# Unread transposes in the first blocks of the two feed-forward layers, with another order of products, splits from the bank and later norms of the memory

## Chip, cores and metric

The kernel runs on one core of a Trainium2 chip. The metric is the device time of one execution in microseconds (us). Before the change the median of three runs is 1266.1 us (1265.81 to 1266.46).

## What is computed

One layer of a streaming encoder over 512 tokens (batch 1) with 1024 channels, all in float32. The reference, cut to what matters:

```python
x = x + 0.5 * swiglu(rmsnorm(x, ffn1_norm), ffn1_wg, ffn1_wu, ffn1_wd)      # 1024 -> 2816 -> 1024
h = rmsnorm(x, mix_norm)
aq, ak, av, bq, bk, bv, cq = split(h @ w_in)
o_a = diff_attention(...)            # 4 heads, block-causal
o_b = chunk_band_attention(...)      # 8 heads, band of chunks
mk, mv = split(rmsnorm(mem, mem_norm) @ w_mem_kv)     # 256 memory tokens
o_c = memory_attention(rmsnorm(cq), rmsnorm(mk), mv)
y = sum_i sigmoid(h @ w_gate + b_gate)_i * (o_i @ w_branch_i)
x = x + y @ w_out
x = x + 0.5 * swiglu(rmsnorm(x, ffn2_norm), ffn2_wg, ffn2_wu, ffn2_wd)
x = rmsnorm(x, final_norm)
# swiglu(h, wg, wu, wd) = (silu(h @ wg) * (h @ wu)) @ wd
```

## The kernel before, in words

**Three matmuls for one.** Every float32 operand is split into a rounded part (`hi`, a cast on ACT, L77) and the rest (`lo`, a subtraction on DVE, L78). `split` (L75) issues both. A product is then three matmuls on TensorE (PE): hi by hi, lo by hi, hi by lo. So each 128x1024 block of weights costs one ACT cast and one DVE subtraction before PE can finish with it.

**Seven products for eight.** The two up-projections of a feed-forward layer (`ffn`, L346) go by Strassen-Winograd: for a pair of 128-wide slices of wg and wu (an `Item`, L376) and the two halves of the tokens there are seven products of half the size, named 1 to 7. `mm7` (L364) is one of them: 24 matmuls of 256 columns (L373) in two halves j of 12. The weight operand of products 5, 6, 7 and 3 is a sum or difference of weight blocks (`quarter`, made on DVE in `prep`, L390). The token operand is M1 to M7, made once per layer: M1 and M2 are the first 256 tokens (two halves of the channels), the others need the last 256 tokens too. Product 6 accumulates in bank s on top of product 1, then 7, then 4; product 5 goes into bank p or o (`z`), and 3 on top of it. Between them ACT copies bank s out (`snap`, L415 to L418), DVE adds (`cc`, L422), ACT applies silu (`sg`, L431), DVE multiplies (`pr`, L433), and `done` (L435) splits the gated result into `gh` and `gl`.

**The tokens at the start of a layer.** `Operands.rows` (L191) takes one tile of 128 tokens: a reciprocal root on POOL (`rsqrt`, L117), two norm halves on DVE (`xn`, L141), eight transposes on PE into two banks t (L201), and two ACT copies to `raw` (L202). For tiles 0 and 1, `combine` (L205) splits raw into M1 and M2; for tiles 2 and 3 it makes half of M6 (L220, L221 on DVE and a split). `need` (L225) makes M5, M7, M4 and M3 at the first product that wants them. In ffn1, `raw` lies in the tiles `gh` and `gl`, which is why rows of the first block name them.

**Order.** A scheduler sets the order on each engine from the order in which the code issues. `run_jobs` (L334) issues products and slices of the down-projection as jobs: `prep` (DVE, ACT, loads) runs ahead of the product by up to six weight blocks. The 22 slices of the hidden width go in chunks of 4, 6, 6 and 6 (L470), each of them up-projection and then down-projection (`mms`, L503), and `run_jobs` is called for every chunk (L536). PE's order is held only within one job, so the scheduler may mix matmuls of neighbouring jobs. The first block of a layer (chunk 0, first item) goes 1, 2, 1', 2', 6, 5, 7, 4, 3, 6', 5', 7' (the second item's products have a dash).

**The start and the memory.** 32 transposes of the identity that nobody reads (L279 to L281) keep PE at work before the first tokens come. `mem_rows` (L551) loads the 256 memory tokens, norms and transposes them; the scheduler takes loads and norms of it into ffn1's first block. After ffn1, `rows_product` (L584) forms mk, cq and mv; mk's product and mv's take the two banks s in turn, `norm4` (L604) norms mk from its bank on DVE with a root on POOL, and `heads_T` (L611) transposes it. Products with `w_u` of the next stage are prepared in the same time (`wlo` 128x768).

Of the kernel before, what the change touches and what calls it, by code (L numbers as in the profile page):

```python
# [32 lines left out]
PLAN_C0 = "p2 c.qt p2 c.sc p2 f4 c.sc2 p3 f2 c.qt f2 c.pt f4 c.pv"  # L33
# [5 lines left out]
WARM = 32  # L39

# [7 lines left out]
def layer_kernel(ctx: ExitStack, tc: tile.TileContext, a: dict, out: bass.AP):  # L48
# [103 lines left out]

    def norm_T(src, ss, gain, h, t):

        ms = tiny("ms", 1)
        nc.vector.tensor_scalar(out=ms, in0=ss[:, 0:1], scalar1=EPS, scalar2=ss[:, 1:2], op0=ALU.add, op1=ALU.add)
        rs = rsqrt(ms)
# [27 lines left out]
    class Operands:  # L185
# [5 lines left out]
        def rows(self, src, ss, gain, t):  # L191
            ms = tiny("ms", 1)
            nc.vector.tensor_scalar(out=ms, in0=ss[:, 0:1], scalar1=EPS, scalar2=ss[:, 1:2], op0=ALU.add, op1=ALU.add)
            rs = rsqrt(ms)
            xn = scratch("xn")
            for dh in range(2):
                norm_half(xn, src, rs, gain, dh)
                ps = bank("t")
                for k in range(4):
                    c = (dh * 4 + k) * P  # L200
                    nc.tensor.transpose(ps[:, k * P:(k + 1) * P], xn[:, c:c + P], ident)  # L201
                nc.scalar.copy(out=self.raw[dh][:, :, t * P:(t + 1) * P], in_=k4(ps))  # L202
            self.combine(t)

        def combine(self, t):  # L205
            M, (r0, r1) = self.M, self.raw
# [6 lines left out]
            if t < 2:  # L213
                part(1, r0[:, :, cols], cols)
                part(2, r1[:, :, cols], cols)
                return
# [27 lines left out]
    def squares(src):  # L244
        ss = tiny("ss", 2)
        dump = scratch("sq")
        for dh in range(2):
            d = slice(dh * 512, dh * 512 + 512)
            square_half(src[:, d], dump[:, d], ss[:, dh:dh + 1])
        return ss  # L250
# [11 lines left out]
    for t in range(NT):  # L262
        nc.sync.dma_start(out=x_sb[:, t, :], in_=x_v[:, t, :])
        if t == 0:
            gain1 = load_gain("ffn1_norm")
        elif t < 3:
            w1_raw.append(load(a["ffn1_w1"][0, t - 1], 1024))
# [10 lines left out]

    warm = bank("s")  # L279
    for _ in range(WARM):  # L280
        nc.tensor.transpose(warm[:, 0:P], ident, ident)  # L281
# [46 lines left out]
    class Job:  # L328


        def __init__(self, prep, run, blocks=1):
            self.prep, self.run, self.blocks = prep, run, blocks
# [12 lines left out]

    def ffn(pre, x_sb, ops, fp, after, raws=None, before_last=None, after_half=None):  # L346
# [17 lines left out]
        def mm7(ps, blk, m, first):  # L364

            for j in range(2):
                c = slice(j * HS, (j + 1) * HS)
                for k in range(4):
                    o = slice((j * 4 + k) * P, (j * 4 + k + 1) * P)
                    st, mv = tuple(w[:, o] for w in blk), tuple(v[:, k, :] for v in M[m])  # L370
                    for n, (x, y) in enumerate(((st[0], mv[0]), (st[0], mv[1]), (st[1], mv[0]))):

                        nc.tensor.matmul(ps[:, c], lhsT=x, rhs=y, start=first and j + k + n == 0,  # L373
                                         stop=k == 3 and n == 2, skip_group_check=True)

        class Item:  # L376


            def __init__(self, ft, G, g0, raws):
                self.ft, self.G, self.g0 = ft, G, g0  # L380
                self.raws = list(raws or [])
                self.pr = [None, None]

# [6 lines left out]
            def prep(self, p):  # L390
# [4 lines left out]
                if p == 2:  # L395
                    return block(self.raw(1))
                if p == 6:
                    self.s1, self.s2 = quarter(), quarter()
                    add(out=self.s1, in0=self.raw(2), in1=self.raw(3), op=ALU.add)
                    add(out=self.s2, in0=self.s1, in1=self.raw(0), op=ALU.subtract)  # L400
                    return block(self.s2)
                if p == 5:
                    got = block(self.s1)
                    self.s4 = quarter()
                    add(out=self.s4, in0=self.raw(1), in1=self.s2, op=ALU.subtract)
                    return got
# [59 lines left out]
        def product(item, p):  # L466
            return Job(lambda: item.prep(p), lambda blk: item.run(p, blk))

        ft = 0
        for n, nf in enumerate(CHUNKS):  # L470
            last = n == len(CHUNKS) - 1
            G = [fp.tile([P, 6, S], F32R, tag=t, name=t) for t in ("gh", "gl")]
# [3 lines left out]
            if ft == 0:  # L476

                order += [(items[0], 1), (items[0], 2), (items[1], 1), (items[1], 2)]
            else:
                order += [(items[0], 1), (items[0], 2)]  # L480
            for i, item in enumerate(items):
                order += [(item, 6), (item, 5), (item, 7)]
                if i + 1 < len(items) and not (ft == 0 and i == 0):
                    order += [(items[i + 1], 1)]
                if ft == 0 and i == 0:
                    order += [(item, 4), (item, 3)]
                elif i + 1 < len(items):
                    order += [(item, 4), (item, 3), (items[i + 1], 2)]
            jobs = [product(*o) for o in order]
# [3 lines left out]
            for dh in range(2):  # L493
# [3 lines left out]
                def chunk(k, d=d):  # L497
# [11 lines left out]
                def banks(acc, dh=dh, z=z, other=other):  # L509
                    acc.extend(bank(t) for t in (("g", "g", "s", other) if dh == 0 else ("s", z, "g", "g")))  # L510

                if dh == 0 or not last:
# [8 lines left out]
                    for k in range(0, nf, 2):  # L521
                        jobs.append(Job(lambda k=k, chunk=chunk: chunk(k), lambda wc, k=k, run=run: run(wc, k)))
                        if dh == 0 and k == 0:
                            jobs += end
                else:
# [10 lines left out]
            run_jobs(jobs, RING)  # L536
# [9 lines left out]
    for t in range(NT):  # L546
        ops.rows(x_sb[:, t, :], squares(x_sb[:, t, :]), gain1, t)

    mix_in = {}

    def mem_rows():  # L551
# [9 lines left out]
        gain = load_gain("mem_norm")  # L561
        for t in range(NMT):
            mt = scratch("mt")
            nc.sync.dma_start(out=mt, in_=a["mem"][t * P:(t + 1) * P, :])
            norm_T(mt, squares(mt), gain, mix_in["mT"], t)
# [7 lines left out]
    ffn("ffn1", x_sb, ops, fp, row_mix, raws=w1_raw, before_last=mem_rows)  # L573
# [49 lines left out]
    mk_ps = rows_product([bank("s") for _ in range(NMT)], mT, a["w_mem_kv"], 0, **mem_w)  # L623
    for t in range(NMT):
        yn = mem_pool.tile([P, 512], F32, tag="mk", name="mk", bufs=3)
        sq = mem_pool.tile([P, 512], F32, tag="mk", name="mksq", bufs=3)
        heads_T(norm4(mk_ps[t], yn, sq, gck), mkT, slice(t * P, (t + 1) * P))
# [4 lines left out]
    for t in range(NT):  # L632
        sq = mem_pool.tile([P, 512], F32, tag="mk", name="cqsq", bufs=3)
        norm4(cq_ps[t], c_rows[:, t, :], sq, gcq)

    lam = mem_pool.tile([P, 512], F32, tag="mk", name="lam", bufs=3)
# [447 lines left out]
    def row_out(t, ss):  # L1084
        ms = tiny("ms", 1)
        nc.vector.tensor_scalar(out=ms, in0=ss[:, 0:1], scalar1=EPS, scalar2=ss[:, 1:2], op0=ALU.add, op1=ALU.add)
        rs = rsqrt(ms)
# [66 lines left out]
```

## Time and profile before

| | |
|---|---|
| median of three runs | 1266.1 us (1265.81 to 1266.46) |
| the profiled execution | 1268.73 us |
| its span, first to last instruction | 1266.9 us |
| PE busy | 1228.1 us, 97% |
| DVE busy | 843.0 us, 67% |
| ACT busy | 596.8 us, 47% |
| mean granted clock of PE | 0.986 of full speed |

A view of the trace counts from the span's first instruction. Busy time of PE is the time in which a matmul is under way, whether the clock is at full or at half speed; the granted clock (PEclk) says which. In a row of the timeline stand start, duration, engine, line, operation, output<-inputs and, in brackets, how long the engine had been idle before and what released it. Back-to-back matmuls overlap, so what one costs is the distance from its start to the next one's start.

### The profile page before, as it was taken

The numbers are of one execution on the slowest core, as the hardware profiler recorded it, in microseconds if no ns is written. First come the engines' busy times: TensorE is split into PE (matmuls) and PEld (weight loads), VectorE is DVE, ScalarE is ACT, GpSimd is POOL, SyncE is SP. The second block draws the span as 40 slices with busy tenths as digits, with TensorE's granted clock in tenths as the row PEclk, the third lists the DMA queues.
The fourth block names the chain that finished last, engine by engine and source line by source line (L and its number), as shares of the span: only waits on it lengthen the run. The fifth ranks groups of instructions, "written<-read, shape, count | busy, mean of one in ns | idle before, by whom it ended". The sixth has DMA issues, their size and how long they took to land.

```text
span 1266.9 us, 19640 instructions
## 1 busy us (share of the span) xinstructions
PE 1228.1 (97%) x7808; PEld 1119.2 (88%) x7808; DVE 843.0 (67%) x1377; ACT 596.8 (47%) x1115; POOL 106.2 (8%) x108
## 2 busy tenths in 40 slices
PE   7889999999999899999999999999989999999997
PEld 7779989989987799999999999888887998998996
DVE  7977667667664756667765664554697776766753
ACT  7534525435443455554554544442464452542543
POOL 1100000000000301111121121111000000000002
PEclk8899999999999899999999999999989999999999
DMA  6532423323333413212221321145143242332311
GB/s 222 174 103 82 135 84 107 127 79 122 102 123 117 123 39 109 88 42 84 88 88 54 93 88 38 63 146 186 34 135 115 70 134 97 101 125 76 123 44 67
DMA packets 53084, 127.57 MB, mean 101 GB/s; under 512 B 10112, under 2 KB 10624, under 8 KB 52992
## 3 DMA queue, kind: packets, MB, share of 16 engines
q1 hardware_dynamic: 52416, 125.27, 31.1%
q8 instruction: 61, 1.00, 0.3%
q10 hardware_dynamic: 576, 1.05, 0.2%
q14 instruction: 31, 0.25, 0.1%
HBM read 122.11 MB, written 4.19 MB: 100 GB/s over the span
## 4 chain that ended last, share of the span: by engine, by line
PE 91%; DVE 4%; ACT 1%; DMA 1%; POOL 1%; issue 1%; SPq 0%; POOLq 0%; DVEq 0%; ACTq 0%
PE ps_s L373 19%; PE ps_g L110 9%; PE ps_g L112 9%; PE ps_g L111 9%; PE ps_o L373 5%; PE ps_p L110 5%; PE ps_p L112 5%; PE ps_p L111 4%; PE ps_p L373 4%; PE ps_g L373 4%; PE ps_s L110 3%; PE ps_s L111 3%; PE ps_s L112 3%; PE ps_o L906 2%; PE ps_s L874 2%; PE ps_t L722 1%
## 5 line engine op out<-in xcount | busy, mean ns | idle before, releaser
L77 ACT CAST whi<-wraw 128x1024 fp32r<-128x1024 f32 (+1 forms) x120 | 119.1, 993 | 144.6 <-PE ps_s L373 74.1
L78 DVE TENSOR_TENSOR wlo<-wraw,whi 128x1024 fp32r<-128x1024 f32 (+1 forms) x120 | 137.9, 1151 | 67.8 <-ACT whi L77 65.1
L373 PE MATMUL ps_s<-mhi,whi 128*128 128x256 f32 x496 | 140.3, 283 | 8.1 <-ACT snap L417 7.9
L373 PE MATMUL ps_s<-mlo,whi 128*128 128x256 f32 x496 | 139.3, 281 | 0.0
L373 PE MATMUL ps_s<-mhi,wlo 128*128 128x256 f32 x496 | 138.3, 281 | 0.6 <-DVE wlo L78 0.6
L373 PEld LDWEIGHTS ps_s<-mhi,whi 128*128 128x128 f32 x496 | 94.6, 191 | 10.6 <-ACT snap L417 9.5
L77 ACT CAST whi<-quarter 128x1024 fp32r<-128x1024 f32 x54 | 56.8, 1052 | 96.4 <-PE ps_o L112 22.4
L373 PEld LDWEIGHTS ps_s<-mlo,whi 128*128 128x128 f32 x496 | 94.7, 191 | 0.9 <-DVE mlo L78 0.2
L373 PEld LDWEIGHTS ps_s<-mhi,wlo 128*128 128x128 f32 x496 | 94.5, 191 | 0.9 <-DVE wlo L78 0.8
L110 PE MATMUL ps_p<-whi,hh 128*128 128x384 f32 (+1 forms) x264 | 95.0, 360 | 0.0
L112 PE MATMUL ps_p<-whi,hl 128*128 128x384 f32 (+1 forms) x264 | 89.6, 340 | 0.0
L111 PE MATMUL ps_p<-wlo,hh 128*128 128x384 f32 (+1 forms) x264 | 89.0, 337 | 0.0
L78 DVE TENSOR_TENSOR wlo<-quarter,whi 128x1024 fp32r<-128x1024 f32 x54 | 66.0, 1222 | 23.9 <-ACT whi L77 23.9
L110 PE MATMUL ps_g<-hh,fh 128*128 128x512 f32 x192 | 78.1, 407 | 0.0
L112 PE MATMUL ps_g<-hh,fl 128*128 128x512 f32 x192 | 75.5, 393 | 0.1
L111 PE MATMUL ps_g<-hl,fh 128*128 128x512 f32 x192 | 74.9, 390 | 0.0
L859 DVE CAST kx<-ps_t 128x256 fp32r<-128x256 f32 x32 | 13.6, 425 | 84.6 <-PE ps_t L857 84.6
L121 POOL TENSOR_TENSOR rsh<-msh,mhalf 128x4 f32<-128x4 f32 x38 | 45.2, 1191 | 277.5 <-DVE msh L127 225.8
L78 DVE TENSOR_TENSOR fl<-wraw,fh 128x768 fp32r<-128x768 f32 x48 | 50.0, 1042 | 24.0 <-ACT fh L77 24.0
L77 ACT CAST fh<-wraw 128x768 fp32r<-128x768 f32 x48 | 39.9, 833 | 37.7 <-PE ps_g L111 22.4
L724 ACT COPY pT<-ps_t 128x512 f32<-128x512 f32 (+3 forms) x56 | 23.5, 452 | 69.3 <-PE ps_t L722 69.3
L110 PEld LDWEIGHTS ps_p<-whi,hh 128*128 128x128 f32 x264 | 50.4, 191 | 1.6
(416 smaller groups left out, 3691.7 us busy)
## 6 DMA issues: line engine op xcount, KB each, us to landing
wraw<-in_ffn_w SPq DMA_DIRECT2D x88, 512.0 KB, 3.8
wraw<-in_ffn_wd SPq DMA_DIRECT2D x44, 512.0 KB, 3.9
wraw<-in_w_u SPq DMA_DIRECT2D x32, 384.0 KB, 3.2
wraw<-in_w_gb SPq DMA_DIRECT2D x32, 384.0 KB, 3.1
wraw<-in_w_gf SPq DMA_DIRECT2D x16, 384.0 KB, 3.1
wraw<-in_w_mem_kv SPq DMA_DIRECT2D x8, 512.0 KB, 4.1
wraw<-in_w_out SPq DMA_DIRECT2D x8, 512.0 KB, 4.8
x_sb<-in_x SPq DMA_DIRECT2D x4, 512.0 KB, 7.0
```

What stands on the lines that cost most here:

```text
L77: nc.scalar.copy(out=hi, in_=raw)
L78: (engine or nc.vector).tensor_tensor(out=lo, in0=raw, in1=f32(hi), op=ALU.subtract)
L110: nc.tensor.matmul(ps, lhsT=st[0], rhs=mv[0], start=first, stop=False)
L111: nc.tensor.matmul(ps, lhsT=st[0], rhs=mv[1], start=False, stop=False)
L112: return nc.tensor.matmul(ps, lhsT=st[1], rhs=mv[0], start=False, stop=last)
L121: nc.gpsimd.tensor_tensor(out=rs, in0=ms, in1=mhalf[:, :n], op=ALU.pow)
L373: nc.tensor.matmul(ps[:, c], lhsT=x, rhs=y, start=first and j + k + n == 0, stop=k == 3 and n == 2, skip_group_check=True)
L722: nc.tensor.transpose(ps[:, j * P:(j + 1) * P], pt[:, j * P:(j + 1) * P], ident)
L724: nc.scalar.copy(out=pT[:, :n * P], in_=ps[:, :n * P])
L859: nc.vector.tensor_copy(out=un.kx[:, :, qs], in_=heads(p2[:, 0:256], 2))
L874: nc.tensor.matmul(out_, lhsT=q, rhs=k, start=j == 0, stop=j == 1)
L906: nc.tensor.matmul(o[:, vs], lhsT=pT[:, j * P:(j + 1) * P], rhs=un.v[:, j, vs], start=j == 0, stop=j == i)
```

## The change

1. `busy(ps, n)` issues n transposes of the identity into a bank that the next product overwrites. With `BUSY = 16` it stands after each of the first two token tiles of ffn1, and ahead of product 5 of the first item in both feed-forward layers.
2. For token tiles 0 and 1, M1 and M2 are split straight from the transposes' bank, and the copy to `raw` comes after it.
3. The sum of squares of a token tile is one ACT instruction of 1024 elements, not two of 512.
4. The first loads go x0, x1, gain, first weights, x2, second weights, x3; before, gain came ahead of x1.
5. The memory's norms become `mem_norms`, a job behind the products of chunk 1 that loads through the ring of weight buffers; `mem_rows` only transposes.
6. All chunks of a layer are one list of jobs under one written order for PE. The first block goes 1, 2, 1', 2', first half of 5, 6, second half of 5, 7, 6', 4, 3, 5', 7'. Product 1 of chunk 1 is put in behind the first jobs of chunk 0's down-projection. The last half of a chunk's down-projection takes its banks in another order.
7. In the memory's section mv's product goes to the banks t, mk's transposes stand behind it, and the scratch tiles have tags of their own. `PLAN_C0`, the table that mixes pieces of the next stage, has another order.

```diff
+    def busy(ps, n):
+        for _ in range(n):
+            nc.tensor.transpose(ps[:, 0:P], ident, ident)
...
         def rows(self, src, ss, gain, t):
...
-                nc.scalar.copy(out=self.raw[dh][:, :, t * P:(t + 1) * P], in_=k4(ps))
-            self.combine(t)
+                cols = slice(t * P, (t + 1) * P)
+                if t < 2:
+                    split(k4(ps), *(v[:, :, cols] for v in self.M[1 + dh]))
+                nc.scalar.copy(out=self.raw[dh][:, :, cols], in_=k4(ps))
+            if t >= 2:
+                self.combine(t)
...
     def run_jobs(jobs, ring):
         made = alive = 0
-        for n, job in enumerate(jobs):
-            while made < len(jobs) and (made <= n or alive + jobs[made].blocks <= ring):
-                alive += jobs[made].blocks
-                jobs[made].got = jobs[made].prep() if jobs[made].prep else None
-                made += 1
-            with tc.manual_schedule(engines={mybir.EngineType.PE}):
+        with tc.manual_schedule(engines={mybir.EngineType.PE}):
+            for n, job in enumerate(jobs):
+                while made < len(jobs) and (made <= n or alive + jobs[made].blocks <= ring):
+                    alive += jobs[made].blocks
+                    jobs[made].got = jobs[made].prep() if jobs[made].prep else None
+                    made += 1
                 job.run(job.got)
-            alive -= job.blocks
+                alive -= job.frees
...
+                elif p == "5a":
+                    self.z = bank("p" if self.ft // 2 % 2 else "o")
+                    busy(self.z, BUSY)
+                    mm7(self.z, blk, 5, True, (0,))
+                elif p == "5b":
+                    mm7(self.z, self.blk5, 5, False, (1,))
...
+                order += [(items[0], "5a"), (items[0], 6), (items[0], "5b"), (items[0], 7), (items[1], 6), (items[0], 4),
+                          (items[0], 3), (items[1], 5), (items[1], 7)]
...
+                    jobs.insert(hole, product(items[0], 1))
...
-                    acc.extend(bank(t) for t in (("g", "g", "s", other) if dh == 0 else ("s", z, "g", "g")))
+                    acc.extend(bank(t) for t in (("g", "g", "s", other) if dh == 0 else (z, "g", "g", "s")))
...
-            run_jobs(jobs, RING)
             ft += nf
...
+    with tc.manual_schedule(engines={mybir.EngineType.PE}):
+        for t in range(2):
+            ops.rows(x_sb[:, t, :], squares(x_sb[:, t, :]), gain1, t)
+            busy(warm, BUSY)
...
+    def mem_norms():
+        gain = load(a["mem_norm"].partition_broadcast(P), 1024)
+        mix_in["mn"] = []
+        for t in range(NMT):
+            mt = load(a["mem"][t * P:(t + 1) * P, :], 1024)
+            xn = scratch("mn")
+            rs = mean_rsqrt(squares(mt, xn))
+            for dh in range(2):
+                norm_half(xn, mt, rs, (gain[:, :512], gain[:, 512:]), dh)
+            mix_in["mn"].append(xn)
...
-        heads_T(norm4(mk_ps[t], yn, sq, gck), mkT, slice(t * P, (t + 1) * P))
+        mk.append(norm4(mk_ps[t], yn, sq, gck))
...
-    mv_ps = rows_product([bank("s") for _ in range(NMT)], mT, a["w_mem_kv"], 512, **mem_w)
+    mv_ps = rows_product([bank("t") for _ in range(NMT)], mT, a["w_mem_kv"], 512, **mem_w)
...
+    for t in range(NMT):
+        heads_T(mk[t], mkT, slice(t * P, (t + 1) * P))
```

Three places of the order. First, PE from the last slices of the output projection (bank s, `yh`) into the first product of ffn2 (`mhi`, `whi`), with the transposes of its token tiles (`norms`), before:

```order
L112 MATMUL ps_s<-whi,yl 128x512
L201 MATMUL ps_t<-ident,norms 128x128 x16
L373 MATMUL ps_s<-mhi,whi 128x256 x2
L373 MATMUL ps_s<-mlo,whi 128x256
L373 MATMUL ps_s<-mhi,wlo 128x256
```

and with the change (lines left out between the parts are matmuls of the same products):

```order
L113 MATMUL ps_s<-whi,yl 128x512
L207 MATMUL ps_t<-ident,norms 128x128 x8
L381 MATMUL ps_s<-mhi,whi 128x256
L381 MATMUL ps_s<-mlo,whi 128x256
L381 MATMUL ps_s<-mhi,wlo 128x256
...
L381 MATMUL ps_g<-mlo,whi 128x256
L207 MATMUL ps_t<-ident,norms 128x128 x8
L381 MATMUL ps_g<-mhi,wlo 128x256
...
L207 MATMUL ps_t<-ident,norms 128x128 x8
L381 MATMUL ps_s<-mhi,whi 128x256
```

Of the sixteen transposes that stood ahead of the first product, the eight of token tile 2 now stand behind all 24 matmuls of it and two of the next; tile 3's stand behind the second product.

Second, DVE in the same stretch (`raw` is the copy of the transposed tokens, `quarter` a sum of weights or of tokens), before, from the split of tile 1's M2 on:

```order
L78 TENSOR_TENSOR mlo<-raw_9405,mhi 128x4x128
L220 TENSOR_TENSOR raw_9404<-raw_9404 128x4x128
L141 SCALAR_TENSOR_TENSOR norms<-x_sb,rs,norms 128x512 x2
L221 TENSOR_TENSOR quarter<-raw_9405,raw_9404 128x4x128
L400 TENSOR_TENSOR quarter<-quarter,wraw 128x1024
L78 TENSOR_TENSOR mlo<-quarter,mhi 128x4x128
L405 TENSOR_TENSOR quarter<-wraw,quarter 128x1024
L220 TENSOR_TENSOR raw_9404<-raw_9404 128x4x128
L221 TENSOR_TENSOR quarter<-raw_9405,raw_9404 128x4x128
L78 TENSOR_TENSOR flo<-wraw,fhi 128x1024
```

and with the change:

```order
L79 TENSOR_TENSOR mlo<-ps_t,mhi 128x4x128 x2
L158 TENSOR_SCALAR ms<-sst 128x1
L142 SCALAR_TENSOR_TENSOR norms<-x_sb,rs,norms 128x512 x2
L226 TENSOR_TENSOR raw_9162<-raw_9162 128x4x128
L227 TENSOR_TENSOR quarter<-raw_9163,raw_9162 128x4x128
...
L226 TENSOR_TENSOR raw_9162<-raw_9162 128x4x128
L79 TENSOR_TENSOR wlo<-quarter,whi 128x1024
L227 TENSOR_TENSOR quarter<-raw_9163,raw_9162 128x4x128
L242 TENSOR_TENSOR raw_9162<-raw_9163,raw_9162 128x4x256
L79 TENSOR_TENSOR flo<-wraw,fhi 128x1024
```

The norm halves of tile 3 now stand ahead of tile 2's subtraction (L226), and `flo`, which the fourth product needs, stands behind one more split and one more subtraction of 1024 elements.

Third, DVE in the memory's section, where `mk` is the first read of mk's bank, `rsh` POOL's root, before:

```order
L78 TENSOR_TENSOR mwl<-wraw,mwh 128x1024
L127 TENSOR_SCALAR msh<-hss 128x4
L78 TENSOR_TENSOR wlo<-wraw,whi 128x768
L602 TENSOR_TENSOR mk<-ps_s,rsh 128x512
L600 TENSOR_REDUCE hss<-mksq 128x4
```

and with the change:

```order
L79 TENSOR_TENSOR wlo<-wraw,whi 128x768
L128 TENSOR_SCALAR msh<-hss 128x4 x2
L79 TENSOR_TENSOR mwl<-wraw,mwh 128x1024
L646 TENSOR_REDUCE hss<-cqsq 128x4
L648 TENSOR_TENSOR mk<-ps_s,rsh 128x512
```

PE no longer needs mk's bank for mv's product; it needs the splits `mwl` of mv's weights, of which the third stands here and the fourth six rows further, behind four of the norms.
## Rows read from the trace of the kernel before

**Rows 1.** The page: the span, and busy time (share) xinstructions of each engine

```profile
span 1266.9 us, 19640 instructions
...
PE 1228.1 (97%) x7808; PEld 1119.2 (88%) x7808; DVE 843.0 (67%) x1377; ACT 596.8 (47%) x1115; POOL 106.2 (8%) x108
```

**Rows 2.** Windows in us: their length, busy time (xstarts) by engine, PEclk, DMA, GB/s

```profile
1.30:6.50 5.20, 5.15 (x24) 5.15 (x25) 0.44 (x2) 2.04 (x5) 0.56 (x1) 1.00 0.88 267
6.50:8.00 1.50, 1.50 (x14) 1.31 (x13) 1.41 (x2) 0.08 (x1) 0.00 (x0) 1.00 1.02 418
10.00:20.00 10.00, 5.64 (x27) 5.02 (x28) 8.96 (x13) 10.00 (x21) 2.01 (x3) 0.67 0.83 320
30.00:40.00 10.00, 5.67 (x27) 4.60 (x26) 9.56 (x12) 5.40 (x9) 4.86 (x1) 0.70 0.35 106
412.70:419.60 6.90, 4.68 (x11) 3.78 (x12) 4.87 (x10) 1.20 (x2) 2.75 (x3) 0.51 0.48 167
920.00:930.00 10.00, 6.83 (x56) 6.63 (x55) 9.89 (x12) 8.69 (x11) 0.00 (x0) 0.91 0.16 52
930.00:940.00 10.00, 9.68 (x63) 9.47 (x62) 10.00 (x12) 4.79 (x6) 0.00 (x0) 0.75 0.50 159
```

**Rows 3.** PE's waits: releaser: us in total, times, longest

```profile
PE ps_s L110 <- DVE mk L602: 5.8, 1, 5.8
...
PE ps_o L373 <- DVE mlo L78: 3.5, 2, 3.2
```

**Rows 4.** Timeline of DVE in ffn1's first block: the memory's norms

```profile
34.91 1.42 DVE L141 SCALAR_TENSOR_TENSOR xn<-mt,rs,gain 128x512 f32<-128x512 f32 x2 [0.44 <-POOL rs L121]
...
44.44 1.42 DVE L141 SCALAR_TENSOR_TENSOR xn<-mt,rs,gain 128x512 f32<-128x512 f32 x2 [0.44 <-POOL rs L121]
```

**Rows 5.** Timeline of PE in ffn1's first block

```profile
35.81 1.94 PE L149 MATMUL ps_t<-ident,xn 128*128 128x128 f32 x8 [1.23 <-DVE xn L141]
38.12 0.58 PE L373 MATMUL ps_o<-mlo,whi 128*128 128x256 f32 x1 [0.36 <-DVE mlo L78]
...
41.05 0.28 PE L373 MATMUL ps_o<-mhi,whi 128*128 128x256 f32 x1
41.16 0.28 PE L373 MATMUL ps_o<-mlo,whi 128*128 128x256 f32 x1
```

**Rows 6.** Timeline of PE in the memory's section

```profile
414.92 0.77 PE L110 MATMUL ps_s<-mwh,mh 128*128 128x512 f32 x1 [5.78 <-DVE mk L602]
```

**Rows 7.** Timeline of DVE in the memory's section

```profile
412.22 0.96 DVE L78 TENSOR_TENSOR wlo<-wraw,whi 128x768 fp32r<-128x768 f32 x1
414.08 0.69 DVE L602 TENSOR_TENSOR mk<-ps_s,rsh 128x512 f32<-128x512 f32 x1 [0.91 <-POOL rsh L121]
```

**Rows 8.** Timeline of PE at the start of ffn2

```profile
913.41 0.38 PE L373 MATMUL ps_s<-mhi,whi 128*128 128x256 f32 x1 [0.23 <-ACT ps_s L137]
...
928.85 0.58 PE L373 MATMUL ps_o<-mlo,whi 128*128 128x256 f32 x1 [3.17 <-DVE mlo L78]
```

**Rows 9.** Timeline of DVE at the start of ffn2

```profile
914.50 0.69 DVE L220 TENSOR_TENSOR raw<-raw 128x512 f32<-128x512 f32 x1
915.10 1.41 DVE L141 SCALAR_TENSOR_TENSOR norms<-x_sb,rs,norms 128x512 f32<-128x512 f32 x2
...
921.30 1.22 DVE L78 TENSOR_TENSOR flo<-wraw,fhi 128x1024 fp32r<-128x1024 f32 x1
```

**Rows 10.** Timeline of ACT at the start of ffn2

```profile
913.76 1.08 ACT L202 COPY raw<-ps_t 128x512 f32<-128x512 f32 x2
```

**Rows 11.** Timeline of DVE at the end of ffn1's chunk 1

```profile
165.04 0.69 DVE L422 TENSOR_TENSOR cc<-ps_o,snap 128x512 f32<-128x512 f32 x1
...
166.78 0.69 DVE L78 TENSOR_TENSOR gl<-pr,gh 128x512 fp32r<-128x512 f32 x1
```

**Rows 12.** Timeline of ACT at the end of ffn1's chunk 1

```profile
165.49 0.62 ACT L77 CAST gh<-pr 128x512 fp32r<-128x512 f32 x1
166.01 0.41 ACT L431 ACTIVATE sg<-cc 128x256 f32<-128x256 f32 x1
```

More of the change, by code (lines that the diff above doesn't have):

```diff
@@ L191, in rows @@
         def rows(self, src, ss, gain, t):
-            ms = tiny("ms", 1)
-            nc.vector.tensor_scalar(out=ms, in0=ss[:, 0:1], scalar1=EPS, scalar2=ss[:, 1:2], op0=ALU.add, op1=ALU.add)
-            rs = rsqrt(ms)
+            rs = mean_rsqrt(ss)
             xn = scratch("xn")
@@ L242, in need, with squares @@
                 split(hi[1], *self.M[3])
[L244 to L249, printed above, removed]
+    def squares(src, dump=None):
+        ss = tiny("ss", 1)
+        square_half(src, scratch("sq") if dump is None else dump, ss)
         return ss
@@ L277, in layer_kernel @@
     nc.vector.memset(mhalf, -0.5)
+    def busy(ps, n):
+        for _ in range(n):
+            nc.tensor.transpose(ps[:, 0:P], ident, ident)
     warm = bank("s")
-    for _ in range(WARM):
-        nc.tensor.transpose(warm[:, 0:P], ident, ident)
+    busy(warm, WARM)
     def add_rows(x_sb, acc, t, dh, scale, after=None, after_half=None, sss={}):
@@ L362, in block, with mm7 @@
             return weight(None, 1024, fp, (("fhi", "flo"), ("ohi", "olo"))[n - 4], 1, raw=raw)
-        def mm7(ps, blk, m, first):
-            for j in range(2):
+        def mm7(ps, blk, m, first, parts=(0, 1)):
+            for j in parts:
                 c = slice(j * HS, (j + 1) * HS)
@@ L396, in prep @@
                     return block(self.raw(1))
+                if self.s1 is None:
+                    self.s1 = quarter()
+                    add(out=self.s1, in0=self.raw(2), in1=self.raw(3), op=ALU.add)
                 if p == 6:
-                    self.s1, self.s2 = quarter(), quarter()
-                    add(out=self.s1, in0=self.raw(2), in1=self.raw(3), op=ALU.add)
+                    self.s2 = quarter()
                     add(out=self.s2, in0=self.s1, in1=self.raw(0), op=ALU.subtract)
[L401 to L405, printed above, removed]
+                    got = block(self.s2)
+                elif p == 5:
+                    got = self.blk5 = block(self.s1)
+                if p in (5, 6):
+                    self.done56 += 1
+                    if self.done56 == 2:
+                        self.s4 = quarter()
+                        add(out=self.s4, in0=self.raw(1), in1=self.s2, op=ALU.subtract)
                     return got
@@ L435, in done @@
             def done(self, f):
+                if not self.G:
+                    self.G += [fp.tile([P, 6, S], F32R, tag=t, name=t) for t in ("gh", "gl")]
                 split(self.pr[f], *(v[:, self.g0 + f, :] for v in self.G))
@@ L466, in product @@
         def product(item, p):
+            if p == "5a":
+                return Job(lambda: item.prep(5), lambda blk: item.run(p, blk), 1, 0)
+            if p == "5b":
+                return Job(None, lambda blk: item.run(p, blk), 0, 1)
             return Job(lambda: item.prep(p), lambda blk: item.run(p, blk))
         ft = 0
+        jobs = []
         for n, nf in enumerate(CHUNKS):
             last = n == len(CHUNKS) - 1
-            G = [fp.tile([P, 6, S], F32R, tag=t, name=t) for t in ("gh", "gl")]
+            G = []
             items = [Item(ft + i, G, i, raws if ft + i == 0 else None) for i in range(0, nf, 2)]
@@ L475, in ffn @@
             order = []
-            if ft == 0:
+            if n == 0:
                 order += [(items[0], 1), (items[0], 2), (items[1], 1), (items[1], 2)]
-            else:
[L480 to L489, printed above, removed]
+                order += [(items[0], "5a"), (items[0], 6), (items[0], "5b"), (items[0], 7), (items[1], 6), (items[0], 4),
+                          (items[0], 3), (items[1], 5), (items[1], 7)]
+            else:
+                if n == 1:
+                    jobs.insert(hole, product(items[0], 1))
+                else:
+                    order += [(items[0], 1)]
+                order += [(items[0], 2)]
+                for i, item in enumerate(items):
+                    order += [(item, 6), (item, 5), (item, 7)]
+                    if i + 1 < len(items):
+                        order += [(items[i + 1], 1), (item, 4), (item, 3), (items[i + 1], 2)]
+            jobs += [product(*o) for o in order]
+            if n == 1 and middle:
+                jobs.append(Job(middle, lambda got: None, 0, 0))
             end = [product(items[-1], 4), product(items[-1], 3)]
@@ L495, in ffn, with chunk @@
                 acc = []
-                def chunk(k, d=d):
+                def chunk(k, d=d, w=w):
                     return weight_block(w[k * P:(k + 2) * P, d].rearrange("(k p) d -> p k d", p=P))
@@ L524, in ffn @@
                             jobs += end
+                            hole = len(jobs)
                 else:
@@ L560, in mem_rows @@
         mix_in["mT"] = [p.tile([P, ND, NM], F32R, name=n) for n in ("mh", "ml")]
-        gain = load_gain("mem_norm")
         for t in range(NMT):
-            mt = scratch("mt")
-            nc.sync.dma_start(out=mt, in_=a["mem"][t * P:(t + 1) * P, :])
-            norm_T(mt, squares(mt), gain, mix_in["mT"], t)
+            for dh in range(2):
+                transpose_half(mix_in["mn"][t], *mix_in["mT"], t, dh)
     def row_mix(t, ss):
@@ L571, in row_mix @@
         nc.sync.dma_start(out=x_dram[t * P:(t + 1) * P, :], in_=x_sb[:, t, :])
[L573 removed]
+    ffn("ffn1", x_sb, ops, fp, row_mix, raws=w1_raw, before_last=mem_rows, middle=mem_norms)
     h2, mT = mix_in["h"], mix_in["mT"]
@@ L1084, in row_out @@
     def row_out(t, ss):
-        ms = tiny("ms", 1)
-        nc.vector.tensor_scalar(out=ms, in0=ss[:, 0:1], scalar1=EPS, scalar2=ss[:, 1:2], op0=ALU.add, op1=ALU.add)
-        rs = rsqrt(ms)
+        rs = mean_rsqrt(ss)
         xn = scratch("xn")
```

40 lines of the change are left out of this document (22 added, 18 removed).

## The prediction, made before the change was run

> **What bounds the kernel now.** The page comes first: TensorE (PE) is busy for 1228.1 of 1266.9 us, DVE for 67% [rows 1]. So only some 39 us of waits can be won, together with the time that PE loses at half clock. The windows come next, to find where these lie: at the starts of the two feed-forward layers and in the memory's section. In 30 to 40 us PE is busy for 5.67 of 10 us at a mean clock of 0.70 while DVE is busy for 9.56; in 920 to 940 DVE has next to no pause (9.89 and 10.00 of 10) [rows 2]. In both places DVE is the bound, and PE waits for the `lo` halves it makes. The list of PE's waits gives the largest single ones: 5.8 us for DVE's read of mk's bank, and 3.5 us for `mlo` [rows 3]. Each such wait costs twice, since the clock falls behind it: in 412.7 to 419.6 the mean clock is 0.51, the lower of the two levels (1.2 of 2.4 GHz), and PE's 4.68 busy us there would be about half at full speed [rows 2].
>
> The sum is made against the profiled execution: span 1266.9, its own time 1268.73 us, which is 2.6 above the median of 1266.1. I add differences to the median. A measurement of this kernel tells about 0.2%, 2.5 us, from no change.
>
> **A. First block of ffn1: -4 us (bounds -7 and +2).** Gone from DVE's queue are the memory's norms: two groups of 1.42 us with 0.44 of idle time each before them, 3.7 us [rows 4]. Gone from PE are their eight transposes, 1.94 us with a wait of 1.23 ahead [rows 5], but those lay in a wait for M5's `mlo` anyway. DVE is the bound here, so its 3.7 us are the gain; the better bound adds the half-clock stretch that a shorter wait can spare. The wait at M5 itself doesn't go: half of product 5 now comes before product 6, and up to M5's `mlo` DVE has two operations of 1024 elements more and one group of norms less, so PE still stands there until about 38 us, as now [rows 5].
>
> The 32 unread transposes behind the first tiles: in the opening, 24 of the same kind start within 5.15 us, 0.215 us apart, later ones 0.107 apart [rows 2], so 16 cost 1.7 to 3.4 us. Between 10 and 20 us PE is busy for only 5.64 us [rows 2], so this hides in the waits for DVE's norms and splits; if that cover is gone, up to 3.4 us come out, which is the worse bound. The raw copy behind the split frees bank t later, and ACT, which has no pause between 10 and 20 us [rows 2], makes the second tile's transposes wait for it by a few us; that lies in the same cover. The squares, one ACT operation instead of two, and the order of loads I cost at nothing: the same waits hide them.
>
> **B. Memory's section: -3 us (bounds -6 and 0).** mv's product no longer wants mk's bank, so the 5.78 us wait [rows 6] goes, and with it about 2.3 us of half clock [rows 2]: 8.1 us. What is late next is mv's weights: their splits stand behind `wlo` and the norms in DVE's queue (0.96 and 0.69 us each [rows 7]); with three or four of these ahead I expect 2.5 us of waits. And mk's transposes, now behind mv's product, are followed by cast, `mkl` and the transposes of the queries in one row, with nothing of PE's between; two splits of 0.69 and the casts ahead of them leave 2.5 us. So 8.1 - 5 = 3. At the better bound half of the new waits is hidden, at the worse all gain is given back.
>
> **C. Start of ffn2: +6 us (bounds 0 and +9).** Nothing leaves DVE's queue here (the memory was never in it), but its inputs come later. Tile 2's transposes stood ahead of the first product; now they follow 26 of its matmuls, 0.11 us apart [rows 5], so 2.9 us later: the first product begins at 913.41 [rows 8], the transposes end near 917.4, two raw copies take 1.08 [rows 10], and DVE's first subtraction of tile 2 starts at 918 or so instead of 914.50 [rows 9]. DVE has only the norm halves (1.41) to do meanwhile, which it takes first, less one split (1.22) that is moved behind: it idles for about 2.7 us in a stretch in which it is the bound. Tile 3's transposes stand behind product 2. From them to `flo`, which product 2' needs, there are two copies (1.08), then on DVE 0.69, a split of 1.22, 0.69, 1.22 and `flo` with 1.22 [rows 9, 10]: 6.1 us, of which product 1' covers 24 x 0.113 = 2.7. That is a new wait of 3.4 us in front of the one of 3.17 at M5 [rows 8]; it takes up part of the same lateness, so I count half, 1.7. The 16 unread transposes here cost 1.7 if PE isn't waiting at that moment. 2.7 + 1.7 + 1.7 = 6. At 0 the strict order loses nothing that the later waits don't give back; at +9 nothing overlaps.
>
> **D. Ends of chunks: +4 us (bounds 0 and +6).** Before, the scheduler could mix matmuls of the next jobs into a chunk's end. Now PE goes in the written order: product 3 of the last item, one slice of the down-projection (24 matmuls of 512 columns, at twice the 0.113 of 256 columns [rows 5] 5.4 us), then the slice that reads that item's `gh`. In between stand `cc` 0.69, silu 0.41, a multiplication that I take like silu, the cast 0.62 and `gl` 0.69 [rows 11, 12], 2.8 us, and DVE has up to three blocks of 1.2 us ahead of them for the next products: 6.4 against 5.4, up to 1.0 lost. This happens at the ends of two chunks in each layer, some 3.5 us. At the end of chunk 0 the cover is a single product, 2.7 us, against 2.8 plus one or two blocks: 1.3 to 2.5, twice. Together 6, of which I take 4, since DVE is less loaded at these places than at the starts and may have no block ahead.
>
> Sum: -4 - 3 + 6 + 4 = +3, and 1 us for the half-clock stretch that the new wait in C starts where the old order had PE at work: **+4 us, 1270.1 us.** The clock's own share is bounded by the first and the third rival.
>
> **The rivals.**
> *The other side: the clock no longer falls.* The unread transposes stand exactly where PE waits. In 10 to 20, 30 to 40 and 930 to 940 us the mean clock is 0.67, 0.70 and 0.75 [rows 2], which is 6.6, 6.0 and 5.0 us at the lower level; work done there at full speed would take half, up to 3.3 + 3.0 + 2.5 = 8.8 us less. Then +3 - 8.8 = -5.8, 1260.3 us. It decides by the granted clock: above 0.95 in all three places and this case holds. For it speaks that the clock did rise under such transposes alone [rows 2]; against it, that in two of the three places DVE is busy for over 9.5 of 10 us [rows 2], and a faster PE only waits longer for DVE, and that 16 of them last 1.7 us where the waits last 3 to 6. 0.31.
>
> *Gains and losses cancel.* A and B give 7. If `wlo` and the norms fill DVE's time at the start of ffn2, C is 3, and with D at 4 the sum is 0: 1266 us. DVE's idle time there, under 1 us, would show it. 0.14.
>
> *The clock falls in ffn2.* Two waits of over 3 us in the first block instead of one, each followed by a stretch like that in 930 to 940 at 0.75 [rows 2], which costs some 2.5 us: +4 and +5, 1275 us. For it speaks that behind both long waits of this trace, 5.78 and 3.17 us [rows 6, 8], the clock stood lower. 0.17.
>
> *Unread transposes don't hold the clock.* Then the 48 are merely more instructions: 16 at 0.107 us in front of each of three starts, 1.7 us each where PE isn't waiting. With one of the three uncovered beside the forecast's own, +4 + 1.7, and 1 us more of half clock in ffn1: 1273 us. The opening speaks against it: PE had done nothing but such transposes when their spacing halved from 0.215 to 0.107 us [rows 2]. The Trainium skill bears on this (TensorE: Matmul & The Clock Gate, Part 4, PE-mode transpose): it says that a transpose doesn't count as work for the clock as a matmul does. The trace doesn't agree. 0.08.
>
> My forecast itself has 0.30.
>
> **How the numbers follow.** Slower by over 0.2% (above 1268.6): the forecast, the falling clock and the idle transposes, 0.55. Within 0.2%: 0.14. Faster (below 1263.6): 0.31. The range of 8 in 10 reaches from 1257, which holds the faster rival with A at its better bound, to 1278, which holds the falling clock with C at its bound.
>
> **What would show it.** In the changed profile: no wait of mk's product for `mk` on DVE, and instead waits of 1 to 3 us for `mwl` and for `mkl` or the queries (B). DVE idle for 2 to 3 us before tile 2's subtraction near 916, and PE waiting about 3 us for `flo` (C). Waits for `gh<-pr` on ACT at the ends of chunks, 2 us for chunk 0 (D). PE still waiting some 6 us at product 5's first half in ffn1 with DVE at work (A). Wrong would be a granted clock above 0.95 in all three windows, which gives the first rival. Below 0.70 in ffn2's first 30 us it gives the third.

## The result, and the profile after

The changed kernel takes 1274.21 us (median of four runs, 1271.72 to 1276.37) against 1266.10 before: a ratio of 1.0063 with a 95% interval of 1.0040 to 1.0087, so 8 us slower. A fourth run of before, at 1740.59 us, is a disturbed one and is left out of the median and the ratio. The profiled execution of the change took 1273.86 us; between the two profiled executions the difference is 5.1 us, since the one of before, 1268.73, lies 2.6 above its median.

The page of the changed kernel, which answers to [rows 1], shows 64 matmuls more than before (7872 against 7808). These are the unread transposes: 32 in the opening and 16 ahead of product 5 in each of the two layers. The prediction and the first experiment's expectation say 48, which is a miscount.

```profile
span 1272.2 us, 19760 instructions
...
PE 1235.2 (97%) x7872; PEld 1125.5 (88%) x7872; DVE 845.2 (66%) x1377; ACT 598.5 (47%) x1103; POOL 106.5 (8%) x108
```

Its windows, in the columns of [rows 2]:

```profile
10.00:20.00 10.00, 7.90 (x56) 7.48 (x55) 8.84 (x14) 9.58 (x16) 3.16 (x3) 0.83 0.75 301
30.00:40.00 10.00, 4.32 (x34) 3.89 (x33) 10.00 (x12) 6.42 (x8) 0.00 (x0) 0.79 0.23 69
412.70:419.60 6.90, 5.79 (x26) 4.83 (x27) 6.90 (x13) 2.32 (x4) 5.53 (x5) 1.00 0.68 219
920.00:930.00 10.00, 7.25 (x38) 6.97 (x37) 10.00 (x11) 9.51 (x12) 0.00 (x0) 0.66 0.50 153
930.00:940.00 10.00, 9.90 (x86) 9.70 (x85) 10.00 (x12) 4.54 (x7) 0.00 (x0) 1.00 0.01 6
```

The granted clock is higher than before in 10 to 20, 30 to 40 and 930 to 940 us, but lower in 920 to 930 (0.66, before 0.91), and PE is busy for less of 30 to 40 than before. The waits of PE in the changed kernel, which answer to [rows 3]:

```profile
PE ps_o L381 <- DVE mlo L79: 5.5, 1, 5.5
PE ps_g L111 <- ACT gh L78: 4.6, 4, 2.0
PE ps_s L381 <- DVE wlo L79: 4.3, 2, 3.3
PE ps_g L381 <- DVE flo L79: 2.7, 1, 2.7
PE ps_t L661 <- DVE mkl L79: 2.6, 1, 2.6
...
PE ps_t L112 <- DVE mwl L79: 1.5, 1, 1.5
```

The wait for `mk` is gone, and so are the 7.9 us for `snap`. In their place stand `gh` at the ends of chunks, `flo` and `wlo` in ffn2's first block, `mkl` and `mwl` in the memory's section, and a longer one for M5's `mlo` in ffn1.

**Where the time went.** To compare stages in kernels whose order differs, I add up PE's matmuls by their cost at full speed, which is the spacing of their starts in the traces (0.2275 us for 512 columns, 0.173 for 384, 0.1148 for 256, 0.109 for 128, 0.111 for 64; the unread transposes count nothing), and ask when each kernel has done the same amount. The table gives what each stage added against before (us; minus is faster). The edges are at 81, 94, 406, 912, 970, 987 and 1196 us of the kernel before; what lies past the last edge, up to 0.8 us, is left out. The kernels are those of the next section.

| kernel | ffn1 first block | ffn1 end of chunk 0 | ffn1 rest | memory, attention | ffn2 first block | ffn2 end of chunk 0 | ffn2 rest | sum |
|---|---|---|---|---|---|---|---|---|
| the change | -3.8 | +1.4 | +2.1 | -0.7 | +1.5 | +2.5 | +2.2 | +5.1 |
| no_unread | -3.0 | +1.5 | +1.5 | -1.1 | +2.1 | +2.4 | +2.4 | +5.7 |
| old_order_mixed | -3.9 | -0.9 | +0.4 | -0.7 | -1.0 | +0.2 | +0.3 | -5.5 |
| new_order_mixed | +3.0 | -0.8 | +0.4 | +1.1 | +1.3 | +0.2 | +0.3 | +5.6 |
| old_order_written | -0.7 | +1.4 | +2.0 | +0.1 | +1.8 | +4.0 | +1.6 | +10.2 |
| ends_mixed | -3.7 | -0.8 | +0.4 | +1.1 | +2.6 | +0.1 | +0.3 | -0.1 |
| no_bank_split | +0.4 | +2.6 | +1.9 | -2.0 | +0.9 | +3.8 | +1.7 | +9.3 |
| old_memory | -4.3 | +1.4 | +2.0 | +1.5 | +2.0 | +2.4 | +2.1 | +7.1 |
| late_norms_alone | -3.8 | -1.2 | 0.0 | +0.2 | -1.1 | 0.0 | 0.0 | -5.9 |
| split_alone | +0.5 | 0.0 | 0.0 | +0.4 | +1.7 | +1.1 | 0.0 | +3.7 |
| memory_alone | -0.4 | 0.0 | 0.0 | +1.8 | +0.6 | +1.1 | 0.0 | +3.1 |
| late_norms_and_memory | -3.2 | -1.2 | 0.0 | -2.1 | -2.1 | +1.3 | 0.0 | -7.3 |

A step of up to about 1 us in such a table can come from the run alone: in `late_norms_alone` PE, DVE and ACT run the same order as before from 900 to 1000 us, and its column for ffn2's first block shows -1.1; the granted clock in 930 to 940 us is 1.00 there, 0.75 before. The ends of the chunks are the columns "end of chunk 0" and "rest": 1.4 + 2.1 + 2.5 + 2.2 = 8.2 us, more than the whole loss of 5.1 in these two executions.

### The profile page after: what moved, and what is told of

It reads as the page before. It is cut to its first block, busy times and chain, and to the rows that moved or that the text cites. A ratio compares the mean times of both kernels' runs of the same rounds, so it can differ in the third digit from the quotient of the medians.

```text
span 1272.2 us, 19760 instructions
## 1 busy us (share of the span) xinstructions
PE 1235.2 (97%) x7872; PEld 1125.5 (88%) x7872; DVE 845.2 (66%) x1377; ACT 598.5 (47%) x1103; POOL 106.5 (8%) x108
## 4 chain that ended last, share of the span: by engine, by line
PE 86%; DVE 8%; DMA 3%; issue 1%; ACT 1%; POOL 0%; SPq 0%; POOLq 0%; DVEq 0%; ACTq 0%
PE ps_s L381 18%; PE ps_g L111 9%; PE ps_g L113 8%; PE ps_g L112 8%; PE ps_o L381 5%; PE ps_p L111 4%; PE ps_p L113 4%; PE ps_p L112 4%; PE ps_g L381 4%; PE ps_p L381 4%; PE ps_s L113 2%; PE ps_s L111 2%; PE ps_s L112 2%; PE ps_o L955 2%; PE ps_s L923 2%; DVE wlo L79 1%
## 5 line engine op out<-in xcount | busy, mean ns | idle before, releaser
L381 PE MATMUL ps_s<-mhi,wlo 128*128 128x256 f32 x512 | 143.7, 281 | 4.3 <-DVE wlo L79 4.3
L381 PE MATMUL ps_s<-mhi,whi 128*128 128x256 f32 x512 | 144.0, 281 | 0.3 <-ACT mhi L78 0.2
L381 PE MATMUL ps_s<-mlo,whi 128*128 128x256 f32 x512 | 143.6, 280 | 0.3 <-DVE mlo L79 0.3
L381 PEld LDWEIGHTS ps_s<-mhi,wlo 128*128 128x128 f32 x512 | 97.4, 190 | 4.7 <-DVE wlo L79 4.7
L381 PEld LDWEIGHTS ps_s<-mhi,whi 128*128 128x128 f32 x512 | 97.8, 191 | 1.2 <-ACT mhi L78 0.5
```

## The experiments

Ratios are to the kernel before, timed beside each of these kernels, with 95% intervals.

**1. Without the unread transposes** (`no_unread`).

```diff
-BUSY = 16
+BUSY = 0
```

> The change without its 48 unread transposes (the 32 at the very start stay). My theory: they stand in waits and neither cost nor save much; the loss of 8 us is made by PE's written order. Then 1272 to 1276 us, with the same waits for flo, wlo and gh in ffn2 as in the change. Rival 1: they are the loss (up to 3.4 us at each of three places): 1266 to 1270. Rival 2: they hold the clock up and save time: over 1277, with longer stretches at the lower clock in both first blocks.

Measured: 1274.69 us, ratio 1.0060 (1.0048 to 1.0073), the change's own. Its windows show what they do:

```profile
10.00:20.00 10.00, 4.90 (x22) 4.14 (x21) 9.23 (x14) 9.23 (x16) 2.15 (x3) 0.64 0.74 297
30.00:40.00 10.00, 5.39 (x38) 4.99 (x36) 10.00 (x12) 7.99 (x10) 0.00 (x0) 0.83 0.36 120
920.00:930.00 10.00, 5.79 (x33) 5.29 (x32) 10.00 (x10) 9.51 (x12) 0.00 (x0) 0.83 0.45 157
930.00:940.00 10.00, 9.70 (x70) 9.70 (x71) 10.00 (x12) 3.09 (x5) 0.00 (x0) 0.83 0.01 2
```

In the opening the clock without them is 0.64, with them 0.83; over all kernels it is 0.55 to 0.67 in the six without the opening's 32 and 0.83 to 1.00 in the seven with them. But DVE is busy for 9.23 to 10 us of each 10, and a faster PE waits for it all the same: ffn1's first block gains 3.0 without them and 3.8 with them. So in the opening they move the clock and next to nothing of the time. In ffn2 they don't move the clock either: over 920 to 950 us its mean is 0.83 with and without them.

**2. Old order of the first block, jobs mixed by the scheduler** (`old_order_mixed`), **3. only mixed** (`new_order_mixed`), **4. only the old order** (`old_order_written`). Mixed means:

```diff
-        with tc.manual_schedule(engines={mybir.EngineType.PE}):
-            for n, job in enumerate(jobs):
...
-                job.run(job.got)
+        for n, job in enumerate(jobs):
...
+            with tc.manual_schedule(engines={mybir.EngineType.PE}):
+                job.run(job.got)
```

and the old order, which drops product 5's 32 unread transposes with it,

```diff
-                order += [(items[0], "5a"), (items[0], 6), (items[0], "5b"), (items[0], 7), (items[1], 6), (items[0], 4),
-                          (items[0], 3), (items[1], 5), (items[1], 7)]
+                order += [(items[0], 6), (items[0], 5), (items[0], 7), (items[0], 4), (items[0], 3),
+                          (items[1], 6), (items[1], 5), (items[1], 7)]
```

> The change with two things of its order undone: the first block goes 6, 5, 7, 4, 3, 6', 5', 7' again (so product 5's unread transposes go too), and PE's order is held within one job only, so the scheduler mixes neighbouring jobs. Splits from the bank, late norms, the memory's section and the one list of jobs stay. My theory (the written order loses 8 us at the start of ffn2 and at the ends of chunks, the rest gains 3 to 5): 1261 to 1266 us, no wait for gh over 0.6 us at a chunk's end. Rival (the splits from the bank or the memory's section are the loss): 1272 or more.

> The change with PE's order held within one job only, so that the scheduler mixes neighbouring jobs; the first block keeps its new order of products. If the strict order across jobs is the cause by itself (the waits for gh at the ends of chunks go, the rest stays): 1266 to 1269 us. If the new order of the first block loses as much by itself: 1270 to 1273, with the gain of 4 us in ffn1's first block gone.

> The change with the first block of each layer in the order 6, 5, 7, 4, 3, 6', 5', 7' (without product 5's unread transposes), PE still strictly in written order. If the new order of the first block is the cause by itself: 1264 to 1268 us. If the strict order is: 1272 to 1278, with waits for snap in the first blocks (before they were 7.9 us in all) on top of those for gh.

| | PE in written order | jobs mixed |
|---|---|---|
| new order of the first block | 1274.2 (the change) | 1273.8, 1.0059 (1.0045 to 1.0073) |
| old order | 1278.8, 1.0105 (1.0091 to 1.0119) | 1265.3, 0.9989 (0.9980 to 0.9999) |

Neither half is the cause by itself; together they are. Undoing both gives 9 us back. Mixing alone gives nothing: the four columns of the ends go from 8.2 to 0.1 in sum, but the first block of ffn1, in the new order, from -3.8 to +3.0, and the memory's and attention's column from -0.7 to +1.1. My guess of 1270 to 1273 for that case was a little low. And the old order in strict sequence is the worst: PE stands for 11.0 us at `mlo`, as its waits show.

```profile
PE ps_s L381 <- DVE mlo L79: 11.0, 3, 5.8
PE ps_s L381 <- ACT mhi L78: 5.1, 3, 4.1
PE ps_g L111 <- ACT gh L78: 4.0, 2, 2.0
```

**5. The first block as in the change, everything behind it mixed** (`ends_mixed`): the first 13 jobs of a layer stay under one written order, later ones are held job by job.

> The change with PE's written order across jobs kept for the first block only (the first 13 jobs of a layer); from there on PE's order is held within one job, as before, so the ends of the chunks may be mixed. My theory (term D: the ends of the chunks lose 5 to 7 us because PE reaches gh before it is made): 1265 to 1269 us, no wait for gh over 0.6 us, ffn1's first block as in the change. Rival (the first block's own order is the loss, the waits for gh only stand where others would): 1272 to 1275.

Measured: 1269.21 us, ratio 1.0018 (1.0009 to 1.0027), 5 us under the change and 0.2 above the upper edge of my range. Its waits:

```profile
PE ps_o L391 <- DVE mlo L79: 5.7, 1, 5.7
PE ps_s L391 <- DVE wlo L79: 3.2, 1, 3.2
PE ps_g L391 <- DVE flo L79: 2.7, 1, 2.7
```

These are the change's own waits of the first blocks, and no wait for `gh` at a chunk's end is left in the list. The four columns of the ends add 0.0 us in place of 8.2. This shows term D directly. What remains of the loss is ffn2's first block, +2.6; and the memory's column, which gains 0.7 in the change, loses 1.1 here.

**6. Splits from raw again** (`no_bank_split`), the change otherwise.

```diff
-                cols = slice(t * P, (t + 1) * P)
-                if t < 2:
-                    split(k4(ps), *(v[:, :, cols] for v in self.M[1 + dh]))
-                nc.scalar.copy(out=self.raw[dh][:, :, cols], in_=k4(ps))
-            if t >= 2:
-                self.combine(t)
+                nc.scalar.copy(out=self.raw[dh][:, :, t * P:(t + 1) * P], in_=k4(ps))
+            self.combine(t)
```

> The change with the splits of the first two tiles from raw again, as before. In its order all sixteen transposes of tiles 1 and 2 stand ahead of ffn2's first product again. If my term C was right in its mechanism (tile 2's late transposes idle DVE at the start of ffn2): 1269 to 1272 us, DVE without idle time in 914 to 919. Rival (DVE's work, not its inputs, sets the time there; what the late transposes cost is given back at M5, and ffn1 loses its earlier splits): 1273 to 1278.

Measured: 1276.92 us, ratio 1.0084 (1.0067 to 1.0101): the rival. All sixteen transposes stand ahead of the first product, DVE no longer waits for the raw copy, and counted from the start of tile 1's transposes (908.86 in the change, 913.41 here) its subtraction comes after 3.5 us in place of 6.2. But other work of DVE moves behind it, and PE gets `flo` after 15.2 us in both. DVE in the change,

```profile
912.19 1.42 DVE L142 SCALAR_TENSOR_TENSOR norms<-x_sb,rs,norms 128x512 f32<-128x512 f32 x2 [0.66 <-POOL rs L122]
915.08 0.69 DVE L226 TENSOR_TENSOR raw<-raw 128x512 f32<-128x512 f32 x1 [1.48 <-ACT raw L211]
...
922.83 1.22 DVE L79 TENSOR_TENSOR flo<-wraw,fhi 128x1024 fp32r<-128x1024 f32 x1
```

and without the splits from the bank,

```profile
915.68 1.29 DVE L79 TENSOR_TENSOR mlo<-raw,mhi 128x512 fp32r<-128x512 f32 x2 [0.43 <-ACT mhi L78]
916.89 0.69 DVE L226 TENSOR_TENSOR raw<-raw 128x512 f32<-128x512 f32 x1
...
919.52 1.41 DVE L142 SCALAR_TENSOR_TENSOR norms<-x_sb,rs,norms 128x512 f32<-128x512 f32 x2
```

where the norms of tile 3 come after the subtraction. PE waits 2.6 us for `flo` there, 2.7 in the change. In ffn1 the splits from the bank are worth 4 us within the new order: its first block goes from -3.8 to +0.4 without them.

**7. The memory's section as before** (`old_memory`): mv's product in the banks s, `heads_T` right behind `norm4`; the new `PLAN_C0` and the scratch tiles' own tags stay.

> The change with the memory's section as before: mv's product into the banks s and mk's transposes right behind mk's norm. My theory (the section gained 1.3 us by the trace): 1275 to 1278 us, with the wait for mk of some 5 us back. Rival (the new section loses as much as it gains): 1272 to 1275.

Measured: 1276.87 us, ratio 1.0078 (1.0065 to 1.0092), as my theory had it. The wait is back, and longer:

```profile
PE ps_s L111 <- DVE mk L648: 7.2, 1, 7.2
```

**8 to 11. Parts alone on the kernel before.** Late norms (`late_norms_alone`: `mem_norms` as a job behind chunk 1's products, `mem_rows` only transposes), the splits from the bank (`split_alone`), the memory's section (`memory_alone`), and late norms, section and `PLAN_C0` together (`late_norms_and_memory`).

> The kernel before with the late norms of the memory and nothing else. My theory (DVE is the bound of ffn1's first block and gets 3.7 us back): 1261 to 1264 us, with the gain complete by 90 us. Rival (the norms lay in waits, the gain in ffn1 comes from the new order): 1265 to 1267.

> The kernel before with the splits of the first two tiles from the bank and nothing else. If it helps by itself: under 1265 us, the first product of ffn1 starting earlier. If the bank is held longer (the raw copies come after the casts, the next tile's transposes wait for them): 1267 to 1270.

> The kernel before with the memory's section changed (mv's product in the banks t, mk's transposes behind it) and nothing else, PLAN_C0 as before. By the two traces the section gains 1 to 2 us: 1264 to 1266 us at the section's end. Rival: the scheduler places later stages otherwise and gives it back: 1266 to 1269, with the loss past 900 us.

> The kernel before with late norms, the new section of the memory and the new PLAN_C0, no other part. If the parts add up (late norms -4.5; the memory's section alone cost 4.5, in the change it gained 1 to 3, so with the new plan -1): 1260 to 1262 us. If the section costs outside of the change too: 1264 to 1268.

| kernel | us | ratio to before |
|---|---|---|
| late_norms_alone | 1262.65 | 0.9961 (0.9948 to 0.9973) |
| split_alone | 1271.79 | 1.0046 (1.0032 to 1.0059) |
| memory_alone | 1269.87 | 1.0036 (1.0022 to 1.0050) |
| late_norms_and_memory | 1261.42 | 0.9961 (0.9949 to 0.9974) |

Late norms do what was expected, in the stage where it was expected (-3.8 by the end of the first block). The other two single parts lose more than I had for either case. `split_alone` wins nothing in ffn1 and loses 1.7 + 1.1 us in ffn2 up to the end of chunk 0. There its PE has the transposes of tile 2 behind the first product, the first row being tile 1's eight:

```profile
910.35 1.03 PE L201 MATMUL ps_t<-ident,norms 128*128 128x128 f32 x8
...
916.24 0.60 PE L201 MATMUL ps_t<-ident,norms 128*128 128x128 f32 x4
```

So their late place comes with the split from the bank, in the old order too. `memory_alone` loses 1.8 us in its own column: with the old `PLAN_C0` PE waits 4.0 us for `mkl`, 2.3 for `mwl` and 1.0 for `cql`, together more than the 5.8 for `mk`. It loses 0.6 + 1.1 more in ffn2, where the change touches nothing; from 933 us on the scheduler has put some instructions of all three engines in another order there, but which of these costs the time is open. With `PLAN_C0` and late norms the column gains 2.1 us. The longest waits that are left in the section are those of the change:

```profile
PE ps_t L633 <- DVE mkl L78: 2.6, 1, 2.6
PE ps_t L111 <- DVE mwl L78: 1.5, 1, 1.5
```

Of all kernels `late_norms_and_memory` has the lowest median, 5 us under before and 13 under the change; its interval is that of the late norms alone, so how much the section adds is not settled by these runs.

## Why the prediction was right, and where not

The direction was right, 1274.2 lies in the range, and the size was half: +4 against +8.

- **A, ffn1's first block, -4:** right, -3.8 in the table; late norms alone give the same -3.8, by DVE's 3.7 us. But in the change the gain also hangs on the splits from the bank (without them +0.4), which I had at nothing. The wait at M5 stands as foretold: 5.5 us.
- **B, the memory's section, -3:** -0.7, with the waits foretold: `mwl` 1.5 (2.5 expected), then `mv` and `mkl`, 1.1 and 2.6 (2.5 expected), 5.2 in all for the 5.0 of the sum. The step that failed is "and with it about 2.3 us of half clock": that was counted as won, and nothing was charged for the half clock behind the new waits, though they are as long. In 406 to 420 us the granted clock rises from 0.76 to 1.00, but in 420 to 430 and in 430 to 440 it falls from 1.00 to 0.91 and 0.74, as the first two rows show. So the half clock only moved, and 5.8 - 5.2 = 0.6 is left. In `late_norms_and_memory`, with the same three waits, the clock falls less there (0.83 and 1.00) and the column gains 2.1. The windows of the change, and PE's three waits in it:

```profile
420.00:430.00 10.00, 6.28 (x35) 5.33 (x34) 9.30 (x20) 4.99 (x8) 2.96 (x2) 0.91 0.38 97
430.00:440.00 10.00, 10.00 (x40) 8.54 (x39) 4.46 (x13) 2.64 (x9) 4.20 (x7) 0.74 0.51 96
```

```profile
413.81 0.50 PE L112 MATMUL ps_t<-mwl,mh 128*128 128x512 f32 x1 [1.46 <-DVE mwl L79]
426.52 0.66 PE L661 MATMUL ps_t<-ident,mk 128*128 128x128 f32 x4 [1.08 <-ACT mv L698]
429.81 1.12 PE L661 MATMUL ps_t<-ident,y_sb 128*128 128x128 f32 x4 [2.64 <-DVE mkl L79]
```

- **C, start of ffn2, +6:** +1.5 in the change, +2.6 with mixed ends. The step that failed is "it idles for about 2.7 us in a stretch in which it is the bound": DVE idles for 0.66 + 1.48 = 2.1 us before the subtraction (of which only the 1.48 is for the late transposes; and the prediction's own terms make 918 - 914.50 - 1.41 + 1.22 = 3.3, not 2.7), but `no_bank_split` takes most of that away, its first block gains no more than the run alone can (+0.9), and the end of chunk 0 loses that again (+3.8 for +2.5). The 1.7 for the unread transposes didn't come either: without them the column stands at +2.1. The wait for `flo` came (2.7 for 3.4), and where the one of 3.17 at M5 stood [rows 8], the unread transposes now run, and 3.3 us come later at `wlo`. PE in the change:

```profile
913.82 1.04 PE L207 MATMUL ps_t<-ident,norms 128*128 128x128 f32 x8
...
924.11 0.58 PE L381 MATMUL ps_g<-mhi,flo 128*128 128x256 f32 x1 [2.75 <-DVE flo L79]
...
928.97 2.44 PE L286 MATMUL ps_o<-ident 128*128 128x128 f32 x16
...
943.61 0.52 PE L381 MATMUL ps_s<-mhi,wlo 128*128 128x256 f32 x1 [3.29 <-DVE wlo L79]
```

- **D, ends of chunks, +4:** 8.2, above the worse bound of 6, and `ends_mixed` shows it to be the strict order. The step that failed is "Together 6, of which I take 4, since DVE is less loaded at these places". The terms, 3.5 and twice 1.3 to 2.5, add up to 6.1 to 8.5, so the 6 was their lower end, and the discount came on top; the measured 8.2 lies within. At chunk 0 PE waits 2.0 us for `gh`, in both layers, within the 1.3 to 2.5 foretold; the rest is small gaps behind `gh` and `gl`, as at the end of chunk 1, where starts are 0.23 apart before and behind, but 0.44, 0.34 and 0.39 where the new halves come in:

```profile
165.44 0.40 PE L113 MATMUL ps_p<-ohi,gl 128*128 128x512 f32 x1
165.88 0.50 PE L111 MATMUL ps_g<-whi,gh 128*128 128x512 f32 x1
166.22 0.40 PE L112 MATMUL ps_g<-wlo,gh 128*128 128x512 f32 x1
166.61 0.50 PE L113 MATMUL ps_g<-whi,gl 128*128 128x512 f32 x1
...
975.13 0.50 PE L111 MATMUL ps_g<-ohi,gh 128*128 128x512 f32 x1 [2.02 <-ACT gh L78]
```

- **The rivals.** The clock did rise in the three windows named, but to 0.83, 0.79 and 1.00, not above 0.95 in all, and without gain: a faster PE waited for DVE. Only the first rise can be put down to the unread transposes: in 30 to 40 and 930 to 940 us `no_unread` has 0.83 both times, and `late_norms_alone`, without any of the 64, has 1.00 in 930 to 940. That unread transposes don't hold the clock is refuted in the opening (0.83 with them, 0.64 without). (In [rows 2] the column shows 1.00 for 1.30 to 6.50 us too; that the clock was still low there is seen from the spacing of 0.215 us alone.) The Trainium skill's rule on transposes (TensorE: Matmul & The Clock Gate, Part 4, PE-mode transpose) would have the same clock in both; the measurement decides against it here. The clock in ffn2 fell as the third rival had it in 920 to 930 (0.66), but over the first 30 us (910 to 940) it is 0.89, as before, and the whole first block lost 1.5 us, so it doesn't carry the difference.

In sum A + B + C + D came out as -3.8 - 0.7 + 1.5 + 8.2 = +5.2 against the +3 foretold. That the two lie so near is luck: B was taken 2.3 us too good, C 4.5 too high and D 4.2 too low, and the last two cancel. The spans differ by 5.3 us (1272.2 - 1266.9). Between the medians it is 8.1, mostly because the profiled execution of before lies 2.6 over its median.

## What to carry to other kernels

Where one engine (DVE here) is the bound, filling the other's waits with unread work moved the clock in one place and the time in none; taking work away from the bound did (3.7 us of norms, 3.8 us). A wait that is replaced by others as long takes its stretch at the lower clock along, so count that on both sides. The strict order over the seams between stages was paid at every seam: count the chain from the last product to its first reader against what PE has to do meanwhile, and don't discount it without a row to show for it. And two halves of an order can each be right only with the other, so undo them one by one and together before naming a cause.

## What the runs showed that I had not expected

Two edits that each lose alone, the splits from the bank (+0.46%) and the memory's section (+0.36%), each seem to gain within the change (without them it is 1276.9 both times, against 1274.2; the intervals overlap, but the columns of their stages go from -3.8 to +0.4 and from -0.7 to +1.5): what they are worth depends on what stands around them. And 64 unread transposes, of which the first 32 lift the clock from 0.64 to 0.83 in 10 us, left the whole time where it was (1274.7 and 1274.2 us).
